# A four-mixer diffusion trunk on one core: a second buffer for the blocks that RWKV inverts, and its small weights packed into 512 columns

## The chip, the core and the metric

The kernel runs on one core of a Trainium2 chip. The metric is the device time of one execution in microseconds (us); lower is better. The engines of the core work side by side, each through its own queue in order: TensorE (PE, with its weight loads as PEld), VectorE (DVE), ScalarE (ACT), GpSimd (POOL), and SyncE (SP), which here issues nearly all DMAs.

## The reference, cut to what matters

Two layers. Each normalizes 1280 tokens (256 of context, 1024 latents; 1024 wide), projects them, and gives the columns to four mixers: S5, RWKV-7, retention (Ret) and gated linear attention (GLA). Each mixer scans the tokens forward and backward, and their outputs go together through an output projection, then an MLP. The change touches RWKV alone:

```
g = jax.nn.sigmoid(glo) @ g_up                                     # rank 64
w_raw = -softplus(-(w0[d] + jnp.tanh(wlo) @ w_up[d])) - 0.5        # rank 32, one per direction d
a = jax.nn.sigmoid(a0[d] + alo @ a_up[d])                          # rank 32
s = s * w_t + (s @ a_t) * b_t + v_t * k_t                          # 4 heads of 64, token by token
```

The kernel does the scan 64 tokens at a time (a chunk). Within a chunk the tokens depend on each other through a triangular matrix that has to be inverted; that is what "the inverse" means below.

## The kernel before, in words

**Stages.** Per layer: a first norm, the input projection together with S5, then the *head stage* (RWKV, Ret, GLA, and three parts of the modulation weights, `ada`), then output projection, second norm and MLP. In the profiled execution the head stage lies at about 461 to 1050 us in the first layer and 2500 to 3055 us in the second. All that the change does lies there.

**RWKV** works on 128 tokens of one direction, a *unit*; two units, one of each direction, make a *pair*, and there are ten pairs a layer (numbered 0 to 9 here). A pair passes through three steps:

- `unit1` (L361): loads the tokens' columns (`rw_zin`), multiplies the 128 rows `lo` with the small weights `rw_up` (L387 to 394; the result goes through ScalarE's tanh into `rw_l1` and `rw_ta`), and ends with the scores, `rw_TE` and `rw_TO`. `gate` (L481) is part of it for some units.
- `inv` (L506): stores the 32x32 diagonal blocks of the scores to DRAM (`rw_S`, L514: two stores from TE, two from TO), loads them back as `rw_B`, each block on four partitions (L518), and solves them in 31 steps on POOL, two instructions each (L527 `rw_tmp`, L528 `rw_Yv`). The result goes out in four stores (L531, `rw_S2`, which the profile writes `rw_S<-rw_Yv`) and comes back in four loads (L534) as `rw_DT`. I call these five kinds of DMA *score stores*, *B load*, *result stores* and *DT loads*.
- `unit2` and `chain` (L538, L582): the products with DT on TensorE, the state pass, the output.

`rw_B` has one buffer: the B load of pair n+1 waits for the last solving step of pair n. `rw_Yv`, `rw_S` and `rw_S2` have two buffers, DT, TE and TO three.

**Order.** `run` (L636) starts a pair every 6 rounds and its second part 12 rounds later, so `unit2` of pair n stands among the work of `unit1` of pair n+2. `merged` (L1996) mixes RWKV, Ret then GLA, and `ada`, each by its share of an estimate of TensorE's time (class `Pe`, L148), which counts a product half when its contraction has at most 64 rows. The tile framework then sets the order of each engine's queue by a model of its own. Both are done when the kernel is built; on the chip every queue runs in that fixed order.

Of the kernel before, what the change touches and what calls it, by code (L numbers as in the profile page):

```python
# [26 lines left out]
def _consts():  # L27
# [44 lines left out]
    dt = (i[None, :] - i[:, None]).astype(f)            # t - s  # L72
# [9 lines left out]
    ang = np.stack([(tt // 64).astype(f)[:, None] * inv, (tt % 64).astype(f)[:, None] * inv], 1)   # [SEQ, 2, 16]  # L82
# [14 lines left out]
# per-layer small parameters, one column block each (layout only)  # L97
# [3 lines left out]
def _cols(a):  # L101
    """[n*128] -> [128, n]"""
    a = np.asarray(a)
    return np.ascontiguousarray(a.reshape(-1, 128).T)
# [19 lines left out]
def lay_s5(inp, i):  # L124
    """[128, 4*512+64]: B (re; im), B (im; re), C (re; im), C (im; re) by state, and d on the diagonal of its group"""
# [11 lines left out]
def lay_rwup(inp, i):  # L137
    wu = np.asarray(inp["rw_w_up"][i])
    au = np.asarray(inp["rw_a_up"][i])
    gu = np.asarray(inp["rw_g_up"][i])  # L140
    z = np.zeros((128, 1280), np.float32)
    z[0:32, 0:512] = wu.transpose(1, 0, 2).reshape(32, 512)
    z[32:64, 512:1024] = au.transpose(1, 0, 2).reshape(32, 512)
    z[64:128, 1024:1280] = gu
    return z


class Pe:  # L148
    """the tensor engine, with an estimate of the time of what it was given (ns)"""
# [18 lines left out]
class K:  # L168
# [29 lines left out]
    def psum(self, **rings):  # L198
        """the banks of PSUM, shared out among kinds of users; b: the others"""
# [16 lines left out]
# ---------------------------------------------------------------- RWKV-7  # L216
def rw_mix(k, j, z, zm, mu, omu):
    """zm = z + mu*(shifted - z) for the 128 columns of tile j; z, zm [128, T]"""
# [42 lines left out]
RW_ROWS = 13            # rows of the spilled columns: v chunks swapped 2, kk 2, r 2, k 2, lo 1, v 2, v reversed by chunk 2  # L261


def rw_store(k, st, sm, omu, zrw, j, zt):
    """token shift of the 128 columns of tile j (zt [128, T]) and what the scans take from them, to DRAM;
    a generator: the parts that need the tensor engine come after the first step"""
# [45 lines left out]
class Rwkv:  # L312
    """zrw: DRAM [128, RW_ROWS, T] as rw_store leaves it; out(p, ps) takes the transposed output of 128 tokens"""

    R, LAT, NP = 6, 12, 3         # rounds between pairs, to their second part, pairs at a time
# [8 lines left out]
    def setup(self):  # L324
# [12 lines left out]
        # states and buffers with fixed zeros  # L337
# [15 lines left out]
        # by chunk: the first direction's output; what the normalized output is multiplied by, and what is added then  # L353
# [7 lines left out]
    def unit1(self, p, d, pr):  # L361
        """elementwise preparation, transposes, scores of 128 tokens in one direction"""
# [17 lines left out]
        def rev(ap):        # [.., 128] reversed in time for the backward direction  # L380
            return ap[..., ::-1] if d else ap

        def v4(ap):         # [128, 2, 128] -> [128, 2, c, 64]
            return ap.rearrange("p a (c t) -> p a c t", c=2)

        l1, ta = t("l1", [128, 2, 128]), t("ta", [128, 2, 128])
        for o, b, x in ((l1, self.w0h, 0), (ta, self.a0h, 512)):  # L387
            pw = k.ps("u1")
            for ti in range(2):
                cs = slice(x + d * 256 + ti * 128, x + d * 256 + ti * 128 + 128)  # L390
                PE.matmul(pw[:, ti * 128:ti * 128 + 128], self.wup[:, cs], lo, start=True, stop=True)
# [3 lines left out]
        # V (scan order, chunks swapped), token-major, into its place beside the chunk updates  # L395
# [11 lines left out]
        ec = self.ec[u["n"] % 2]        # decay from a chunk's start to before and, one column later, after a token  # L407
# [3 lines left out]
        # ar: (r~ 0 | a~ 0 | a~ 1 | r~ 1); a~ in scan order, r~ in natural order within its chunk  # L411
# [1643 lines left out]
```

## Time and profile before

| | us |
|---|---|
| median of 3 runs | 3920.55 (3920.0 to 3921.86) |
| span of the profiled execution | 3930.7 |
| head stage, first layer (461 to 1050) | about 589 |
| head stage, second layer (2500 to 3055) | about 555 |
| PE busy in the span | 3589.8 (91%) |
| POOL busy in the span | 1353.2 (34%) |

The profiled execution is known by its span, from the first to the last instruction; it is 10 us longer than the median, so a difference worked out on it is taken off the median. A busy share over the whole span hides that the stages differ: outside the head stage PE is nearly always busy, inside it is not. In the rows below, `psu` are the PSUM tiles of RWKV's products, `psb` those of most others. A wait in square brackets is the idle time of the engine just before the instruction, and what ended it.

### The profile page before, as it was taken

The numbers are of one execution on the slowest core, as the hardware profiler recorded it, in microseconds if no ns is written. First come the engines' busy times: TensorE is split into PE (matmuls) and PEld (weight loads), VectorE is DVE, ScalarE is ACT, GpSimd is POOL, SyncE is SP. The second block draws the span as 40 slices with busy tenths as digits, with TensorE's granted clock in tenths as the row PEclk, the third lists the DMA queues.
The fourth block names the chain that finished last, engine by engine and source line by source line (L and its number), as shares of the span: only waits on it lengthen the run. The fifth ranks groups of instructions, "written<-read, shape, count | busy, mean of one in ns | idle before, by whom it ended". The sixth has DMA issues, their size and how long they took to land.

```text
span 3930.7 us, 61448 instructions
## 1 busy us (share of the span) xinstructions
PE 3589.8 (91%) x23136; PEld 2973.0 (76%) x23136; DVE 2222.0 (57%) x4654; ACT 1475.3 (38%) x2980; POOL 1353.2 (34%) x2690
## 2 busy tenths in 40 slices
PE   6999888888799999999998999788888799999997
PEld 2998766577687888888886987667677678888885
DVE  5875456667555444444448875555667464444445
ACT  4266345755433111111214365346655332111222
POOL 1541256567431111111111451266676321111112
PEclk8999988787799999999999999898778899999998
DMA  5434575532521111111103434663423411111111
GB/s 184 149 111 145 163 210 141 168 92 61 163 89 33 33 44 33 43 33 44 33 27 120 146 115 144 180 177 112 111 73 96 141 54 49 49 43 43 49 53 43
DMA packets 369241, 372.84 MB, mean 95 GB/s; under 512 B 97360, under 2 KB 313104, under 8 KB 368688
## 3 DMA queue, kind: packets, MB, share of 16 engines
q1 hardware_dynamic: 333600, 343.08, 28.8%
q10 hardware_dynamic: 35344, 25.83, 2.1%
q8 instruction: 183, 3.00, 0.3%
q14 instruction: 114, 0.93, 0.1%
HBM read 285.18 MB, written 83.63 MB: 94 GB/s over the span
## 4 chain that ended last, share of the span: by engine, by line
PE 64%; POOL 9%; DMA 9%; DVE 8%; ACT 5%; issue 3%; SPq 1%; ACTq 0%; DVEq 0%; POOLq 0%
PE psb L161 56%; PE psu L161 5%; POOL rw_Yv L528 3%; POOL rw_tmp L527 3%; DMA rw_B<-rw_S 2%; DMA rw_S<-rw_Yv 1%; PE pss L161 1%; PE psfi L161 1%; DMA ada_w<-in_ada_w_dram 1%; DVE s_W L1158 1%; PE psch L161 1%; DVE n_h L1579 1%; DMA gl_v<-z_gvg 1%; DVE w_lo L1478 1%; DVE zm L223 1%
## 5 line engine op out<-in xcount | busy, mean ns | idle before, releaser
L161 PE MATMUL psb<-hh,w_hi 128*128 128x512 f32 (+1 forms) x1784 | 664.6, 374 | 12.9 <-ACT hh L1951 4.5
L161 PE MATMUL psb<-hl,w_hi 128*128 128x512 f32 (+1 forms) x1784 | 662.5, 372 | 6.5 <-DVE hl L1581 6.5
L161 PE MATMUL psb<-hh,w_lo 128*128 128x512 f32 (+1 forms) x1784 | 659.5, 371 | 0.0
L161 PE MATMUL psb<-mh,w_hi 128*128 128x512 f32 (+1 forms) x1600 | 601.2, 377 | 20.1 <-ACT w_hi L1475 15.3
L161 PE MATMUL psb<-mh,w_lo 128*128 128x512 f32 (+1 forms) x1600 | 598.3, 375 | 6.6 <-DVE w_lo L1478 6.6
L161 PE MATMUL psb<-ml,w_hi 128*128 128x512 f32 (+1 forms) x1600 | 600.5, 375 | 0.0
L1932 DVE SCALAR_TENSOR_TENSOR x<-psb,mod,x 128x512 f32<-128x512 f32 (+1 forms) x640 | 436.9, 694 | 273.8 <-PE psb L161 273.0
L1478 POOL TENSOR_TENSOR w_lo<-w_raw,w_hi 128x1024 fp32r<-128x1024 f32 x84 | 215.0, 2560 | 765.2 <-ACT w_hi L1475 574.8
L1950 DVE TENSOR_TENSOR hr<-hr 128x512 f32<-128x512 f32 x160 | 150.5, 941 | 513.6 <-ACT hr L1949 513.5
L1949 ACT ACTIVATE hr<-psb 128x512 f32<-128x512 f32 x160 | 88.7, 555 | 862.7 <-PE psb L161 861.8
L161 PEld LDWEIGHTS psb<-hh,w_hi 128*128 128x128 f32 x1784 | 338.6, 190 | 77.7 <-issue 6.0
L161 PEld LDWEIGHTS psb<-hl,w_hi 128*128 128x128 f32 x1784 | 338.0, 190 | 72.7 <-DVE hl L1581 11.0
L161 PEld LDWEIGHTS psb<-hh,w_lo 128*128 128x128 f32 x1784 | 337.5, 189 | 61.2 <-issue 1.4
L1952 POOL TENSOR_TENSOR hl<-hr,hh 128x512 fp32r<-128x512 f32 (+1 forms) x80 | 95.3, 1191 | 795.0 <-ACT hh L1951 502.9
L161 PEld LDWEIGHTS psb<-mh,w_hi 128*128 128x128 f32 x1600 | 303.7, 190 | 81.1 <-ACT w_hi L1475 17.4
L161 PEld LDWEIGHTS psb<-mh,w_lo 128*128 128x128 f32 x1600 | 303.3, 190 | 67.9 <-DVE w_lo L1478 8.2
L161 PEld LDWEIGHTS psb<-ml,w_hi 128*128 128x128 f32 x1600 | 303.4, 190 | 60.3 <-issue 2.9
L1475 ACT CAST w_hi<-w_raw 128x1024 fp32r<-128x1024 f32 (+1 forms) x208 | 212.8, 1042 | 317.8 <-PE psb L161 268.5
L527 POOL TENSOR_TENSOR rw_tmp<-rw_Yv,rw_B 128x60 f32<-128x60 f32 (+24 forms) x620 | 206.1, 332 | 198.6 <-DMA rw_B<-rw_S 100.0
L161 PE MATMUL psb<-w_hi,hh 128*128 128x256 f32 (+1 forms) x928 | 266.0, 290 | 4.8 <-ACT w_hi L1475 4.7
L161 PE MATMUL psb<-w_lo,hh 128*128 128x256 f32 (+1 forms) x928 | 266.9, 288 | 0.6 <-DVE w_lo L1478 0.6
L161 PE MATMUL psb<-w_hi,hl 128*128 128x256 f32 (+1 forms) x928 | 266.2, 288 | 0.0
(469 smaller groups left out, 6710.2 us busy)
## 6 DMA issues: line engine op xcount, KB each, us to landing
w_raw<-in_mlp_w_dram SPq DMA_DIRECT2D x128, 512.0 KB, 3.6
ada_w<-in_ada_w_dram SPq DMA_DIRECT2D x96, 512.0 KB, 4.4
w_raw<-in_w_in_dram SPq DMA_DIRECT2D x40, 512.0 KB, 5.6
w_raw<-in_w_out_dram SPq DMA_DIRECT2D x32, 512.0 KB, 5.2
rw_zin<-z_rw SPq DMA_DIRECT2D x20, 576.0 KB, 5.9
rw_B<-rw_S SPq DMA_DIRECT2D x20, 512.0 KB
z_rw<-zm SPq DMA_DIRECT2D x14, 640.0 KB, 3.1
x<-in_xT_dram SPq DMA_DIRECT2D x4, 2048.0 KB
```

Of the source, the lines that this page charges most:

```text
L161: return self.t.matmul(out, lhsT, rhs, **kw)
L223: nc.vector.scalar_tensor_tensor(dst[p0:p1], src[p0:p1], mu[p0:p1, j:j + 1], dst[p0:p1], op0=OP.mult, op1=OP.add)
L527: eng.tensor_tensor(o, bc(Yv[:, 0:m, s:s + 1], [128, m, n]), bc(B[:, s:s + 1, s + 1:32], [128, m, n]), op=OP.mult)
L528: eng.tensor_tensor(Yv[:, 0:m, s + 1:32], Yv[:, 0:m, s + 1:32], o, op=OP.add)
L1158: T_ = lambda o, a, b, op: V.tensor_tensor(o, a, b, op=op)
L1475: nc.scalar.copy(hi[:, :n], raw[:, :n])
L1478: e.tensor_tensor(lo[:, :n], raw[:, :n], hi[:, :n].bitcast(F32), op=OP.subtract)
L1579: nc.vector.scalar_tensor_tensor(h, x[:, kt], g[:, kt, cond:cond + 1], r[:, :n], op0=OP.mult, op1=OP.mult)
L1932: V.scalar_tensor_tensor(self.x[b][:, dt_], ps[:, :n], mod[:, 40 + dt_, cnd:cnd + 1], self.x[b][:, dt_], op0=OP.mult, op1=OP.add)
L1949: A.activation(r[:, :n], ps[:, :n], AF.Relu)
L1950: V.tensor_tensor(r[:, :n], r[:, :n], r[:, :n], op=OP.mult)
L1952: (G if j else V).tensor_tensor(hl[:, j, :n], r[:, :n], hh[:, j, :n].bitcast(F32), op=OP.subtract)
```

## The change

Beside comments, docstrings and blank lines that go, the diff is this:

```diff
 def lay_rwup(inp, i):
-    z = np.zeros((128, 1280), np.float32)
-    z[0:32, 0:512] = wu.transpose(1, 0, 2).reshape(32, 512)
-    z[32:64, 512:1024] = au.transpose(1, 0, 2).reshape(32, 512)
-    z[64:128, 1024:1280] = gu
+    z = np.zeros((128, 512), np.float32)
+    z[0:32] = wu.transpose(1, 0, 2).reshape(32, 512)
+    z[32:64] = au.transpose(1, 0, 2).reshape(32, 512)
+    z[64:128, 0:256] = gu
...
     def unit1(self, p, d, pr):
-        for o, b, x in ((l1, self.w0h, 0), (ta, self.a0h, 512)):
-            pw = k.ps("u1")
-            for ti in range(2):
-                cs = slice(x + d * 256 + ti * 128, x + d * 256 + ti * 128 + 128)
-                PE.matmul(pw[:, ti * 128:ti * 128 + 128], self.wup[:, cs], lo, start=True, stop=True)
+        pws = [k.ps("u1"), k.ps("u1")]
+        for ti in range(2):
+            for x, pw in enumerate(pws):
+                cs, s = slice(d * 256 + ti * 128, d * 256 + ti * 128 + 128), slice(32 * x, 32 * x + 32)
+                PE.matmul(pw[:, ti * 128:ti * 128 + 128], self.wup[s, cs], lo[s], start=True, stop=True)
+        for o, b, pw in ((l1, self.w0h, pws[0]), (ta, self.a0h, pws[1])):
             for ti in range(2):
                 c = d * 2 + ti
                 A.activation(rev(o[:, ti]), pw[:, ti * 128:ti * 128 + 128], AF.Tanh, ...
...
     def gate(self, p, zin):
-        PE.matmul(pg[:, 0:256], lo, self.wup[:, 1024:1280], start=True, stop=True)
+        PE.matmul(pg[:, 0:256], lo[64:128], self.wup[64:128, 0:256], start=True, stop=True)
...
     def inv(self, pr):
-        B = w.tile([128, 32, 32], F32, name="rw_B", bufs=1)
+        B = w.tile([128, 32, 32], F32, name="rw_B", bufs=2)
-        tmp = w.tile([128, 256], F32, name="rw_tmp", bufs=1)
+        tmp = w.tile([128, 76], F32, name="rw_tmp", bufs=1)
```

Per partition `rw_B` takes 4096 bytes more, `rw_up` 3072 and `rw_tmp` 720 less. The products with the small weights have 32 rows of contraction in place of 128 (64 in `gate`), so `Pe` counts them half. Line numbers behind L387 grow by one. The order of the queues changes inside the two head stages; three places follow.

SP's queue, first layer, the score stores (`rw_S<-rw_TE`, `rw_TO`) and the B load of pair 4 and the result stores (`rw_S2<-rw_Yv`) of pair 3. Before:

```order
L514 DMA rw_S_7417<-rw_TE_7234 32x8x32 x2
L514 DMA rw_S_7417<-rw_TO_7235 32x8x32 x2
L754 DMA gl_g_8680<-z_gvg0_398 128x256
L917 DMA z_gk0_396<-gl_c_7539 128x257
L917 DMA z_gk0_396<-gl_c_7540 128x257
L899 DMA gl_L_7639<-z_ga0_397 16x256
L917 DMA z_gk0_396<-gl_c_7600 128x257
L917 DMA z_gk0_396<-gl_c_7601 128x257
L899 DMA gl_L_7688<-z_ga0_397 16x256
L518 DMA rw_B_7422<-rw_S_7417 128x1x1024
L531 DMA rw_S2_6840<-rw_Yv_6775 256x1x32 x4
```

The same place in the change:

```order
L515 DMA rw_S_7353<-rw_TE_7161 32x8x32 x2
L515 DMA rw_S_7353<-rw_TO_7162 32x8x32 x2
L519 DMA rw_B_7358<-rw_S_7353 128x1x1024
L607 DMA rw_dY_4776<-rw_Y_7434 128x256
L374 DMA rw_zin_8470<-z_rw0_393 128x9x128
L532 DMA rw_S2_6764<-rw_Yv_6699 256x1x32 x4
```

The B load moved up to its score stores, and other DMAs now stand between it and the result stores of the pair before.

SP's queue, first layer, score stores and B load of pair 8, result stores and DT loads (`rw_DT`) of pair 7. Before:

```order
L514 DMA rw_S_10906<-rw_TE_10648 32x8x32 x2
L514 DMA rw_S_10906<-rw_TO_10649 32x8x32 x2
L518 DMA rw_B_10911<-rw_S_10906 128x1x1024
L531 DMA rw_S2_10188<-rw_Yv_10123 256x1x32 x4
L754 DMA gl_g_10231<-z_gvg0_398 128x256
L799 DMA gl_L_10233<-z_gq0_395 128x128
L534 DMA rw_DT1_4764<-rw_S2_10188 32x8x32 x4
```

The same place in the change:

```order
L532 DMA rw_S2_9918<-rw_Yv_9853 256x1x32 x2
L615 DMA rw_YQ_11098<-rw_dY_4776 128x768
L535 DMA rw_DT1_4764<-rw_S2_9918 32x8x32 x4
L524 DMA rw_Yv_11471<-in_consts_dram 128x256
L755 DMA gl_g_9615<-z_gvg0_398 128x256
L800 DMA gl_L_9617<-z_gq0_395 128x128
L755 DMA gl_c_10028<-z_gk0_396 128x385
L515 DMA rw_S_10632<-rw_TE_10371 32x8x32 x2
L515 DMA rw_S_10632<-rw_TO_10372 32x8x32 x2
L519 DMA rw_B_10637<-rw_S_10632 128x1x1024
```

The score stores and the B load moved behind the result stores and the DT loads of the pair before.

POOL's queue, first layer, the end of the solving steps of pair 7 and the first of pair 8 (`128x31`). Before:

```order
L527 TENSOR_TENSOR rw_tmp_10124<-rw_Yv_10123,rw_B_10121 128x8
L528 TENSOR_TENSOR rw_Yv_10123<-rw_Yv_10123,rw_tmp_10124 128x8
L725 TENSOR_TENSOR gl_nth_9905<-gl_nth_9905,gl_lng_7524 128x256
L527 TENSOR_TENSOR rw_tmp_10914<-rw_Yv_10913,rw_B_10911 128x31
L528 TENSOR_TENSOR rw_Yv_10913<-rw_Yv_10913,rw_tmp_10914 128x31
L808 TENSOR_TENSOR gl_L_10233<-gl_c_10224 128x64
```

In the change, the last of 18 instructions that stand there:

```order
L812 TENSOR_TENSOR gl_L_9617<-gl_c_9608 128x2x32
L809 TENSOR_TENSOR gl_L_9617<-gl_c_9608 128x4x16
L810 TENSOR_TENSOR gl_L_9617<-gl_c_9608 128x4x16
L811 TENSOR_TENSOR gl_L_9617<-gl_c_9608 128x4x16
L812 TENSOR_TENSOR gl_L_9617<-gl_c_9608 128x4x16
L809 TENSOR_TENSOR gl_L_9617<-gl_c_9608 128x8x8
L810 TENSOR_TENSOR gl_L_9617<-gl_c_9608 128x8x8
L811 TENSOR_TENSOR gl_L_9617<-gl_c_9608 128x8x8
L812 TENSOR_TENSOR gl_L_9617<-gl_c_9608 128x8x8
L528 TENSOR_TENSOR rw_tmp_10640<-rw_Yv_10639,rw_B_10637 128x31
```

GLA's elementwise work of one chunk stood between the solving steps of pair 8 and now stands ahead of them.

## Rows read from the trace of the kernel before

**Rows 1.** The page's head, then the chain of waits by line, head stages of both layers

```profile
span 3930.7 us, 61448 instructions
...
by line: PE psu L161 14.6%; POOL rw_tmp L527 7.8%; POOL rw_Yv L528 7.5%; PE psb L161 6.5%; issue 6.1%; DMA rw_B<-rw_S 4.6%; PE psfi L161 4.1%; DMA rw_S<-rw_Yv 4.1%; DMA ada_w<-in_ada_w_dram 3.4%; PE psch L161 2.4%; DMA z_mix<-rw_mix 2.0%; P
...
by line: PE psu L161 16.2%; POOL rw_Yv L528 10.7%; DMA rw_B<-rw_S 10.0%; POOL rw_tmp L527 9.9%; issue 5.9%; PE psb L161 5.3%; DMA rw_S<-rw_Yv 3.6%; DMA rw_DT<-rw_S 2.5%; PE psfi L161 2.5%; PE psch L161 2.2%; DMA gl_v<-z_gvg 2.2%; SPq L531 2
```

**Rows 2.** POOL around the end of inverse 0, in time: start, length, engine, line

```profile
560.67 0.47 POOL L528 TENSOR_TENSOR rw_Yv<-rw_Yv,rw_tmp 128x8 f32<-128x8 f32 x1
...
569.46 0.24 POOL L527 TENSOR_TENSOR rw_tmp<-rw_Yv,rw_B 128x31 f32<-128x31 f32 x1 [5.11 <-DMA rw_B<-rw_S]
```

**Rows 3.** Windows of POOL over gaps between inverses: length, busy (instructions); three sets

```profile
701.94:714.41 12.47, 0.17 (x4) 0.50 0.35 95
...
2637.39:2651.87 14.48, 8.30 (x18) 0.93 0.47 106
...
sum 81.06, POOL 19.07; mean POOL 2.72
...
847.56:864.24 16.68, 4.87 (x17) 0.69 0.35 89
...
sum 47.71, POOL 6.32; mean POOL 1.58
...
sum 68.56, POOL 2.21; mean POOL 0.32
```

**Rows 4.** SP's queue in time: score stores of pairs 1 and 4, B load of 1

```profile
529.51 0.95 SPq L514 DMA_DIRECT2D rw_S<-rw_TO  x2
...
560.62 0.55 SPq L518 DMA_DIRECT2D rw_B<-rw_S  x1
...
683.80 0.89 SPq L514 DMA_DIRECT2D rw_S<-rw_TO  x2
```

**Rows 5.** SP's queue in time: pair 7 after inverse 6; stores after inverse 7

```profile
847.59 2.52 SPq L531 DMA_DIRECT2D rw_S<-rw_Yv  x4
850.15 0.60 SPq L514 DMA_DIRECT2D rw_S<-rw_TO  x1
...
852.70 2.58 SPq L534 DMA_DIRECT2D rw_DT<-rw_S  x4
...
856.29 0.56 SPq L518 DMA_DIRECT2D rw_B<-rw_S  x1
...
900.81 2.81 SPq L531 DMA_DIRECT2D rw_S<-rw_Yv  x4
...
909.83 1.80 SPq L534 DMA_DIRECT2D rw_DT<-rw_S  x4
```

**Rows 6.** Windows by stage: length, PE, PEld, DVE, ACT, POOL busy, granted clock

```profile
510.00:710.00 200.00, 163.22 (x1159) 126.49 (x1159) 117.08 (x313) 103.93 (x270) 131.11 (x342) 0.86 0.54 156
710.00:1010.00 300.00, 264.47 (x3258) 219.47 (x3257) 212.06 (x573) 179.61 (x488) 209.05 (x607) 0.78 0.38 106
2550.00:2750.00 200.00, 173.12 (x1174) 132.65 (x1173) 112.86 (x303) 101.46 (x266) 128.88 (x354) 0.87 0.51 147
2750.00:3030.00 280.00, 233.42 (x2945) 204.78 (x2945) 192.74 (x508) 162.55 (x447) 191.28 (x546) 0.76 0.31 82
```

**Rows 7.** PE in time: small weights (128 rows), then Ret (64 rows), then `ada`

```profile
532.35 0.71 PE L161 MATMUL psu<-rw_zin,rw_up 128*128 128x128 f32 x4
532.99 0.72 PE L161 MATMUL psb<-rt_qt,rt_kt 64*128 64x128 f32 x8
533.64 1.03 PE L161 MATMUL psfi<-ada_w,condsl 128*2 128x512 f32 x4
```

**Rows 8.** The chain of waits in time, start of the head stages

```profile
461.24 3.79 DMA rw_up<-in_rwup_dram
...
2503.19 6.86 DMA rw_zin<-z_rw
```

## The prediction

> **What bounds the kernel now.** I read the page first, then the chain of waits cut to the two head stages, because the diff touches nothing outside them. The page says how long the profiled execution is: 3930.7 us [rows 1]. That is 10 us above the median of 3920.55; every sum below is a difference on the profiled execution and is taken off the median. In the head stages the chain passes through TensorE's RWKV products, the solving steps on POOL (15% and 21% of the stage, two lines each), and a DMA, `rw_B<-rw_S`, with 4.6% and 10.0% [rows 1]. These shares are of windows of 592 and 570 us, so the B load has 27 and 57 us of the chain. This is the most the chain could lose by it, if nothing else were late next.
>
> Then POOL in time. Inverse 0 ends at 561.14 (560.67 + 0.47), inverse 1 starts at 569.46, and its wait is for the B load [rows 2]. SP issued that load at 560.62, although the last score stores of pair 1 were issued at 529.51 [rows 4]: with one buffer it had to wait for the last solving step. So each pair has a gap on POOL in which a 9 us load runs and little else. The 18 gaps between the inverses of both layers come to 197 us (81.06 + 47.71 + 68.56), in which POOL works 28 (19.07 + 6.32 + 2.21) [rows 3]. That idle time, 170 us over both layers, is what is at stake.
>
> Third, the windows by stage: PE is busy 834 of 980 us (163.22 + 264.47 + 173.12 + 233.42) [rows 6]. So PE leaves 146 us; a gain of 170 can't be had, one of 30 to 70 can.
>
> **The change part by part: the second buffer.** It lets the B load start when its own score stores have landed. Whether it does depends on where SP's fixed queue has it, so I sort the 18 gaps by the order of the change and by when the scores come in the trace.
>
> (a) *Seven gaps (before pairs 1, 2, 4 of the first layer, 1, 2, 3, 6 of the second): the load stands ahead of the earlier pair's result stores, and the scores are early.* Pair 1's last score stores leave 31 us before the inverse ahead of it ends [rows 2, 4]; the latest of the seven are pair 4's, 18 us ahead (683.80 against 701.94 [rows 3, 4]). From the last score store to the first solving step pair 7 needs 14.1 us (850.15 of [rows 5] to 864.24 of [rows 3]). So the data are there and the gap closes. Idle now: 81.06 - 19.07 = 62 us [rows 3]. Left: half a microsecond each, and some 5 us before pair 2, half of whose scores now stand behind `unit2` of pair 0 on PE. Gain 62 - 3 - 5 = 54 us. The 19 us of other POOL work in these gaps is still to be done.
>
> (b) *Four gaps (before pairs 5 and 7; 4 and 7): the load stands early, but the scores are late.* Pair 7's last score store leaves at 850.15 [rows 5], the inverse ahead ends at 847.56 [rows 3]; in the other three it leaves at most 12 us ahead. Here the 14 us of stores, load and waits pass whatever the buffer; the idle 47.71 - 6.32 = 41 us [rows 3] stays, moved earlier with the rest. Gain 0, at most 41.
>
> (c) *Seven gaps (before pairs 3, 6, 8, 9; 5, 8, 9): the score stores now stand behind the earlier pair's result stores, four of them behind its DT loads too.* This is the part that speaks against the change. Before, one gap has just this order: pair 7 after inverse 6 (it counts in set (b) by its new place). There the result stores go out at 847.59, the last score store at 850.15, the DT loads at 852.70, the B load at 856.29 [rows 5], and the gap is 16.68 us where the others of set (c) have 68.56 / 7 = 9.8 [rows 3]. For the three that have one pair of score stores ahead of the DT loads I take 16.7; for the four that have both behind them I add those loads and the stores, 2.6 + 1.7, and get 21. Sum 3 x 16.7 + 4 x 21 = 134 us. The order of POOL moves 84 other instructions out of the inverses into these gaps (7, 0, 18, 18; 7, 16, 18); at 0.38 us (8.30 + 4.87 us for 18 + 17 [rows 3]) that is 32 us of work that no longer lengthens an inverse. So idle 134 - 32 = 102 against 68.56 - 2.21 = 66 now: a loss of 36 us. The ends: a loss of nothing if a gap stays at 9.8, of 60 if the result stores take as long to land as after inverse 7 (909.83 - 903.62 = 6.2 us, against 852.70 - 850.11 = 2.6 [rows 5]), since 7 x 3.6 = 25 come on top.
>
> (d) *The results come back sooner.* After inverse 7 the B load was sent just ahead of the result stores, and the DT loads could go 6.2 us after the last of these; after inverse 6, with no B load ahead, after 2.6 [rows 5]. Now no B load is sent at that moment, so `unit2` gets its DT some 3.6 us sooner. It counts where `unit2`, and `unit1` behind it, is what the next inverse waits for: the four gaps of (b) and the two ends of stage, 6 x 3.6 = 22 us. I take 10, since PE has other work queued there; ends 0 and 22.
>
> **The small weights.** Their load is 0.26 MB in place of 0.66. On the chain of the first layer it has 3.79 us [rows 8]; at the same rate 2.3 go. In the second it lies ahead of the chain's 6.86 us load of `rw_zin` [rows 8], and up to as much goes. I take 3 in all. No row shows a product of 32 rows with 128 columns. Four products of 128 rows start 0.64 us before the next group, 160 ns each; the eight 64-row products behind them, two halves of the array by turns, take 0.65, 81 ns each, the change of shape at both ends included [rows 7]. With the 64-row price four take 0.32 less a group; 40 groups give 13 us of PE time. The other end is no gain, or a loss of the same size if two 32-row products don't overlap. Most of it lies where PE has a wait behind it anyway; I take 2.
>
> At this point the Trainium skill speaks against the edit: "TensorEngine Tiling (Array Packing)", Key Properties, says that changing the tiling mode drains the engine, and each of these groups now changes it twice. Here the rows disagree as to size: the 64-row group pays both changes within its 81 ns each. By the rule alone, with a drain of one group's 0.3 us, the 40 groups would lose 12 us of PE time in place of gaining 13.
>
> `gate`'s product keeps its 256 columns and runs alone: nothing. The smaller `rw_tmp` costs nothing; the largest step needs 76 columns. That `Pe` counts less makes RWKV stand a little earlier among Ret, GLA and `ada`; the work is the same.
>
> **The sum.** -54 + 0 + 36 - 10 - 3 - 2 = -33. 3920.55 - 33 = 3888 us.
>
> **The rivals.**
>
> *All gaps close (faster).* If the scores in set (c) are ready only when the queue takes them, their place costs nothing, and the pieces I call late are just PE's own pace: (c) is 0, and (d) counts in full: -54 + 0 - 22 - 3 - 2 = -81, which is over half of PE's 146 idle us; with 20 given back to PE's queue -61, 3860 us. For it: the queue is made with a model in which stores stand when their data come. Against it: before, in every gap of (c) the stores left ahead of the result stores.
>
> *SP's queue becomes the bound (slower).* The result stores of an inverse and the score stores of the next pair are now one chain on SP, and the loads of `rw_zin` for the pair after stand behind them. Price: the late gaps at their far end (-54 + 60), nothing from (d), and the gain of (a) halved since the next pair's scores start later: -27 + 60 = +33, less 5 for the weights: 3948 us. It decides from the point at which the seven gaps average over 24 us: (134 + 33) / 7. For it: SP waits in order, and all other loads with it. Against it: the one gap of this order measured 16.68.
>
> *PE is the bound (no change).* PE is busy 88% of 710 to 1010 [rows 6] and works in order. If its queue there is what is slow, the gains of the second halves are waits that move from POOL to PE, and only pairs 1 and 2 of each layer give something, about as much as (c) takes: 3917 us.
>
> *The change doesn't do what it says*: excluded for the buffer, since in 11 of 18 gaps the load has moved ahead of the result stores.
>
> **How the numbers follow.** Forecast 0.52 (3888, by itself 3868 to 3906), all gaps close 0.18, SP's queue 0.17, PE 0.13. The range goes to the first rival's 3860 and some 10 below, and towards the slower one's until a tenth is left out: 3850 to 3930. Within 0.2% (8 us) counts as no change, which is about what a measurement can tell here. Faster: 0.52 + 0.18 and a little of PE's case, 0.72; same 0.12; slower 0.16.
>
> **What would show it.** Right: the POOL windows of the seven gaps of (a) drop to about 1 us, those of (c) grow to 17 to 21 and hold the other POOL work, and no B load is left on the chain in (a); the wait from the result stores to the DT loads drops to under 3 us; a group of four small products takes about 0.35 us. Wrong: gaps in (c) under 10 (first rival) or above 24 (second), or the gaps of (a) closed and the stage as long as before, with PE's waits for `rw_DT` grown (third).

## The result, and the profile after

The change made the kernel slower: 3975.76 us, median of four runs (3963.14 to 3982.85), against 3921.2 for the kernel before, ratio 1.0135, 95% interval 1.0112 to 1.0159. Forecast were 3888 us and a range up to 3930.

The profiled execution of the changed kernel is 50.4 us longer than that of before:

```profile
span 3981.1 us, 61419 instructions
```

First, windows by stage as in [rows 6], but each span is cut where the load of `rw_up` (start of a head stage) and the first load of the output projection's weights (its end) are issued. The columns are length, busy time of PE, PEld, DVE, ACT and POOL with their instructions, granted TensorE clock, DMA share, GB/s. Before:

```profile
461.20:1051.60 590.40, 491.34 (x4978) 392.56 (x4978) 387.43 (x1035) 320.80 (x863) 371.25 (x1005) 0.81 0.49 142
2499.90:3062.50 562.60, 455.14 (x4430) 372.47 (x4430) 359.71 (x943) 297.23 (x803) 346.94 (x952) 0.81 0.45 126
0.00:461.20 461.20, 413.18 (x2634) 351.01 (x2634) 290.44 (x755) 216.24 (x355) 133.45 (x264) 0.96 0.44 140
1051.60:2499.90 1448.30, 1400.04 (x7606) 1197.51 (x7606) 777.40 (x1429) 434.58 (x684) 314.46 (x372) 0.98 0.23 71
3062.50:3930.70 868.20, 830.12 (x3488) 659.46 (x3488) 407.03 (x494) 206.47 (x275) 187.08 (x101) 0.97 0.18 58
```

and the changed kernel:

```profile
467.00:1094.50 627.50, 518.85 (x4978) 408.37 (x4978) 388.20 (x1034) 318.19 (x859) 364.76 (x1004) 0.77 0.47 131
2534.60:3116.30 581.70, 471.57 (x4430) 381.12 (x4430) 356.86 (x943) 298.39 (x803) 332.30 (x952) 0.75 0.43 121
0.00:467.00 467.00, 415.40 (x2634) 352.98 (x2634) 287.51 (x755) 216.13 (x355) 132.96 (x264) 0.96 0.43 139
1094.50:2534.60 1440.10, 1392.84 (x7606) 1192.67 (x7606) 780.18 (x1430) 435.48 (x686) 314.10 (x372) 0.98 0.23 72
3116.30:3981.00 864.70, 825.28 (x3488) 660.69 (x3488) 407.11 (x494) 206.47 (x275) 186.88 (x101) 0.98 0.18 58
```

The head stages grow by 37.1 and 19.1 us; the rest is +5.8 ahead of them (nothing there is touched, and in five of the other traces the first head stage starts 3.3 to 4.6 us late too) and -8.2 and -3.5 behind them. Look at PE's busy time, the second column. TensorE issues as many instructions as before, 4978 and 4430, yet is busy 27.5 and 16.4 us longer. So 44 of the stages' 56 us is an equal number of instructions that take longer, and the clock says how: 0.81 and 0.81 became 0.77 and 0.75. The clock has two levels, 1.2 and 2.4 GHz, so the mean gives the time at the lower one: 2 x 0.19 x 590.4 = 224 us before, 2 x 0.23 x 627.5 = 289 now; in the second layer 214 and 291. Counted over the traces' records, PE was busy at the lower level for 174 and 166 us before and for 229 and 214 now; half of that growth is 52 us, which covers the 44. PE's idle time grew by 9.6 and 2.7 only.

Second, the gaps between inverses on POOL, which answer to [rows 3], in the sets (a), (b), (c) of the prediction (the last line is the twenty inverses themselves):

```profile
sum 6.20, POOL 0.69; mean POOL 0.10
...
sum 20.93, POOL 5.16; mean POOL 1.29
...
sum 183.68, POOL 26.16; mean POOL 3.74
...
sum 795.15, POOL 596.11; mean POOL 29.81
```

(a) went from 81.06 us to 6.20, as forecast; (b) from 47.71 to 20.93, better; (c) from 68.56 to 183.68, 26.2 each where 19 were forecast. The sum of all three is 210.81 us, where it was 197 before: the gaps moved and grew. This is how such a place looks in SP's queue, to be read beside [rows 5]: the last score store of pair 6 and its B load leave behind the result stores (L532) and DT loads (L535) of pair 5 (one line of each is shown):

```profile
801.21 0.57 SPq L532 DMA_DIRECT2D rw_S<-rw_Yv  x1
...
803.60 1.27 SPq L535 DMA_DIRECT2D rw_DT<-rw_S  x1
...
807.85 0.43 SPq L515 DMA_DIRECT2D rw_S<-rw_TO  x1
...
810.54 0.56 SPq L519 DMA_DIRECT2D rw_B<-rw_S  x1
```

Third, PE's groups in the head stages; behind the bar stand busy time, mean ns of one record (a float32 product leaves two) and the idle time just before. Before, first layer, then second:

```profile
L161 PE MATMUL psu<-rw_R,rw_DT 128*128 128x128 f32 x320 | 55.5, 334 | 24.6 <-DMA rw_DT<-rw_S 22.7 <-DVE rw_R L558 1.9
L161 PE MATMUL psfi<-ada_w,condsl 128*2 128x512 f32 x192 | 49.9, 663 | 8.7 <-DMA ada_w<-in_ada_w_dram 8.6
...
L161 PE MATMUL psu<-rw_R,rw_DT 128*128 128x128 f32 x320 | 62.0, 360 | 31.2 <-DMA rw_DT<-rw_S 31.1
L161 PE MATMUL psb<-gl_v,gl_kt 128*32 128x64 f32 x144 | 6.1, 245 | 3.2 <-DMA gl_v<-z_gvg 2.2 <-ACT gl_mix L1713 0.9
```

The changed kernel:

```profile
L161 PE MATMUL psfi<-ada_w,condsl 128*2 128x512 f32 x192 | 58.8, 685 | 33.9 <-DMA ada_w<-in_ada_w_dram 33.8
L161 PE MATMUL psu<-rw_R,rw_DT 128*128 128x128 f32 x320 | 56.4, 333 | 6.1 <-DMA rw_DT<-rw_S 5.9 <-DVE rw_R L559 0.3
...
L161 PE MATMUL psu<-rw_R,rw_DT 128*128 128x128 f32 x320 | 55.9, 334 | 6.7 <-DMA rw_DT<-rw_S 6.3 <-DVE rw_R L559 0.3
L161 PE MATMUL psb<-gl_v,gl_kt 128*32 128x64 f32 x144 | 6.8, 272 | 20.2 <-DMA gl_v<-z_gvg 12.5 <-ACT gl_mix L1714 6.1 <-ACT gl_kt L764 1.5
```

The gaps that the second buffer was to close are closed, and PE's wait for the DMA of DT fell by 16.8 and 24.8 us, 42 in all. That the buffer did it can be seen in the second layer only: the kernel with the packing and one buffer, below, has this wait at 6.1 and 35.0 us, where it is 5.9 and 6.3 here and was 22.7 and 31.1 before. The wait for `ada`'s weights rose by 25.2 in the first layer and the idle time ahead of GLA's products `gl_v,gl_kt` by 17.0 in the second: PE's queue is in a fixed order, and it stood still at another place. (The chain of waits of this trace breaks off at 3116.87 us, so it can't be set beside [rows 1].)

### The profile page after: what moved, and what is told of

It is laid out like the page before. It is cut to its first block, busy times and chain, and to the rows that moved or that the text cites. A ratio compares the mean times of both kernels' runs of the same rounds, so it can differ in the third digit from the quotient of the medians.

```text
span 3981.1 us, 61419 instructions
## 1 busy us (share of the span) xinstructions
PE 3623.9 (91%) x23136; PEld 2995.8 (75%) x23136; DVE 2219.9 (56%) x4654; ACT 1474.7 (37%) x2978; POOL 1331.0 (33%) x2690
## 5 line engine op out<-in xcount | busy, mean ns | idle before, releaser
L1950 ACT ACTIVATE hr<-psb 128x512 f32<-128x512 f32 x160 | 88.5, 554 | 858.5 <-PE psb L161 857.6
L528 POOL TENSOR_TENSOR rw_tmp<-rw_Yv,rw_B 128x60 f32<-128x60 f32 (+24 forms) x620 | 195.1, 315 | 166.5 <-DMA rw_B<-rw_S 41.5
```

Of the source, the lines that this page charges most:

```text
L528: eng.tensor_tensor(o, bc(Yv[:, 0:m, s:s + 1], [128, m, n]), bc(B[:, s:s + 1, s + 1:32], [128, m, n]), op=OP.mult)
L1950: A.activation(r[:, :n], ps[:, :n], AF.Relu)
```

## The experiments

All were timed against the kernel before on the same chip; its medians there were 3921 to 3928 us. "Clock" is the range of the mean granted clock over the timed runs, "stages" the lengths of the two head stages in the profiled one.

| kernel | us | ratio (95%) | clock | stages |
|---|---|---|---|---|
| changed | 3975.76 | 1.0135 (1.0112, 1.0159) | 0.912 to 0.916 | 627.5, 581.7 |
| packing, one buffer | 3988.04 | 1.0155 (1.0135, 1.0174) | 0.910 to 0.914 | 646.4, 577.1 |
| changed, old cost | 3972.46 | 1.0114 (1.0096, 1.0132) | 0.915 to 0.916 | 638.2, 567.2 |
| results on ACT's queue | 3993.43 | 1.0170 (1.0153, 1.0187) | 0.911 to 0.914 | 635.2, 577.7 |
| results on POOL's queue | 3973.66 | 1.0111 (1.0086, 1.0136) | 0.912 to 0.919 | 625.3, 576.2 |
| before, light cost | 3948.46 | 1.0069 (1.0053, 1.0084) | 0.925 to 0.927 | 613.8, 565.1 |
| before, 32 rows | 3992.37 | 1.0184 (1.0162, 1.0207) | 0.910 to 0.917 | 611.9, 598.7 |
| program order, 128 rows | 4207.58 | 1.0738 (1.0714, 1.0762) | 0.898 to 0.902 | 714.3, 665.6 |
| program order, 32 rows | 4219.10 | 1.0757 (1.0736, 1.0777) | 0.888 to 0.892 | 720.4, 675.9 |

**Which half of the change.** Theories: SP's queue (1), the order that lighter costs bring (2), the 32-row products (3), waits that move from the gaps into the inverses (4). The packing alone, with `rw_B` at `bufs=1` and `rw_tmp` at 256 columns:

> The change without its second buffer (rw_B with one buffer, rw_tmp with 256 columns as before): the packed weights, the 32-row products and the lighter counting of their cost alone. Theory 1 (the harm is SP's in-order queue, where score stores and B loads now stand behind the earlier pair's result stores): with one buffer the B load waits for the last solving step again, the eighteen gaps between inverses sum to about 190 to 215 us and the time is 3915 to 3935 us. Theory 2 (the harm is the order that the lighter costs give, which leaves the last GLA chunks behind the last unit2 at the end of the first layer): the first out-projection is late by 20 us as in the changed kernel, 3940 to 3960. Theory 3 (the 32-row products themselves are slow): 3950 to 3980, with these products at over 160 ns each.

It is as slow as the whole change: the packing alone is enough for the harm, 64 us by the medians. The changed kernel's median is 12 us lower, but the intervals overlap, so that the second buffer gives anything back is not shown. Then the old cost:

```diff
                 PE.matmul(pw[:, ti * 128:ti * 128 + 128], self.wup[s, cs], lo[s], start=True, stop=True)
+                PE.cost += 4 * 128 / 2.4 * 0.5
...
         PE.matmul(pg[:, 0:256], lo[64:128], self.wup[64:128, 0:256], start=True, stop=True)
+        PE.cost += 4 * 256 / 2.4 * 0.5
```

> The changed kernel, but the products with the packed weights and gate's product are counted at their old cost in the merge of RWKV with Ret, GLA and ada, so that it goes nearly as before the change. Theory 1 (SP's queue): 3965 to 3985, late gaps still 24 to 28 us each. Theory 2 (the lighter costs shift the order): 3915 to 3940, the end of the first layer's stage back by about 20 us. Theory 3: as the changed kernel, 3976.

No difference from the changed kernel that the intervals show. (The scheduler's own model still sees other products, so before's order doesn't come back.) Its second stage is worth a look:

```profile
2542.20:3109.40 567.20, 457.85 (x4430) 369.27 (x4430) 356.48 (x943) 299.44 (x805) 338.85 (x952) 0.80 0.45 124
```

With 32-row products the clock there is 0.80 and PE is busy 458 us, where before had 0.81 and 455. Its first stage has 0.74. So the order has a part in what 32-row products cost.

**SP's queue.** The result stores and DT loads go to ScalarE's queue, or the result stores alone to POOL's:

```diff
-            nc.sync.dma_start(S2[:, :, :, j].rearrange("x b i t -> (x b) i t"), Yv[32 * j:32 * j + 32])
+            nc.gpsimd.dma_start(S2[:, :, :, j].rearrange("x b i t -> (x b) i t"), Yv[32 * j:32 * j + 32])
```

> The changed kernel with the result stores and the DT loads issued by ScalarE on its own queue, so that no score store and no B load stands behind them on SP. Theory 1 (SP's queue): the seven late gaps fall from 26 us on average to under 12, some 100 us of gaps go, of which a third to a half reaches the end: 3900 to 3945. Theory 2 (order): gaps fall but the stages end no sooner, 3960 to 3985. Theory 4 (the end of an inverse is set by PE and by POOL's own waits, so that what a gap loses the inverse before or after it gains): the sum of the inverses' own lengths grows by what the gaps lose, 3950 to 3985.

> The changed kernel with the result stores alone issued by POOL, the engine that makes the results; DT loads, score stores and B loads stay on SP, where the B loads then stand early for all pairs. Theory 1 (SP's queue): late gaps under 12 us, 3890 to 3940 us. Theory 2 (order): 3950 to 3985. Theory 4 (waits move into the inverses): 3950 to 3985, the sum of the inverses' lengths above the changed kernel's 795 us by what the gaps lose.

Theory 1 falls: neither is faster. The windows of the second, first over its 18 gaps, then over its 20 inverses:

```profile
sum 122.27, POOL 57.19; mean POOL 3.18
...
sum 878.31, POOL 631.56; mean POOL 31.58
```

The gaps of all sets lost 88.5 us (210.81 in the changed kernel), the inverses grew by 83.2 (795.15 there), as theory 4 has it. Of the 83.2, POOL's own work is 35.5 (631.56 for 596.11) and waiting 47.7. POOL takes its queue in order too, and what it no longer waits for in the gaps it waits for inside the inverses, in part at instructions of other mixers. One of its groups in that kernel between 569.22 and 862.86, idle time behind the bar:

```profile
L1018 POOL TENSOR_TENSOR rt_vd<-rt_v,rt_GV 128x256 f32<-128x256 f32 x4 | 2.5, 614 | 19.9 <-DMA rt_v<-z_ret 19.9
```

This wait was not new: over the first head stage the group waits 33.0 us here, 27.0 in the changed kernel. The late gaps of (c) were not what set the time.

**Order against rows.** The kernel before with the lighter cost only, and the kernel before with only the 32 rows (64 in `gate`) that are not zero, cost restored:

```diff
+                PE.cost -= 4 * 128 / 2.4 * 0.5
```

```diff
-                PE.matmul(pw[:, ti * 128:ti * 128 + 128], self.wup[:, cs], lo, start=True, stop=True)
+                q = slice(0, 32) if x == 0 else slice(32, 64)
+                PE.matmul(pw[:, ti * 128:ti * 128 + 128], self.wup[q, cs], lo[q], start=True, stop=True)
```

> The kernel before, with nothing changed but the estimate: the products with the small weights and gate's product are counted half, as after the change. All 128-row products, the one buffer and the wide weights stay; only the order of the queues moves. Seen so far in all four kernels with packed weights: the head stages have as many TensorE instructions as before (4978 and 4430), but TensorE is busy for 20 to 47 us longer in the first, and its granted clock there is 0.74 to 0.77 where it was 0.81. Theory order (a queue order without the gaps and cover of before's lengthens the stage, and the clock follows): 3945 to 3990, clock in the first head stage under 0.78. Theory rows (products on 32 rows lower the granted clock, whatever the order): 3910 to 3935, clock 0.80 to 0.82.

> The kernel before with its wide weights, one buffer and its loop order, but the products with the small weights take only the 32 rows that are not zero (gate's 64), and are counted at their old cost. The queues still move, since the scheduler's model sees other products. Theory rows: the granted clock in the first head stage is 0.74 to 0.77, 3955 to 3990. Theory order: undecided by itself, as its order is neither before's nor the change's: 3915 to 3990.

The first, by windows of its two stages:

```profile
462.10:1075.90 613.80, 490.13 (x4978) 393.12 (x4978) 386.59 (x1034) 315.31 (x859) 369.94 (x1004) 0.80 0.48 135
2518.00:3083.10 565.10, 450.05 (x4430) 370.52 (x4430) 354.68 (x943) 299.98 (x805) 337.84 (x952) 0.80 0.46 126
```

TensorE's busy time is that of before (490 for 491, 450 for 455) and so is the clock; the stage is 23 us longer by idle time. So order alone costs: the time is what the theory of order gave, the clock what the theory of rows gave. The 32-row kernel, with wide weights and one buffer:

```profile
460.40:1072.40 612.00, 503.70 (x4978) 394.78 (x4978) 389.29 (x1035) 318.61 (x861) 357.39 (x1005) 0.79 0.48 137
2516.40:3115.10 598.70, 472.23 (x4430) 378.36 (x4430) 357.73 (x943) 299.72 (x805) 336.08 (x952) 0.77 0.43 119
```

Its clock is lower, though in the first stage less than the 0.74 to 0.77 that was expected, and of the 58 us by which its stages are longer PE's busy time is 29; the rest is idle time, and its order differs too. To take the order out, the kernel before and this one were built with the queues in the order of the program (`schedule_with_timeline_sim=False`); then every queue of the two is the same, and 178 products differ (four in each of 40 units, and 18 of `gate`; the expectation counts 176 groups):

> The kernel before with its queues in the order in which the program is written, not in the order of the scheduler's model. A base line for the next kernel: 3950 to 4150.

> The products on 32 rows (64 in gate) of the kernel two places ahead, with the queues in the order of the program: every queue has exactly the order of the base line, and only the 176 groups of products with the small weights differ. Theory rows: slower than the base line by 25 to 70 us, granted clock in the head stages lower by 0.03 to 0.07, TensorE busier by 15 to 40 us. Theory order: within 8 us of the base line and the same clock, or faster by up to 13 us.

Windows of the head stages with 128 rows:

```profile
496.30:1210.60 714.30, 515.69 (x4978) 392.29 (x4978) 377.37 (x1031) 321.67 (x861) 357.99 (x1002) 0.77 0.42 117
2685.20:3350.80 665.60, 478.60 (x4430) 377.41 (x4430) 346.54 (x940) 306.76 (x809) 336.30 (x950) 0.75 0.38 106
```

and with 32 rows:

```profile
494.80:1215.20 720.40, 541.65 (x4978) 402.75 (x4978) 377.14 (x1031) 321.99 (x861) 355.64 (x1002) 0.73 0.42 116
2690.50:3366.40 675.90, 498.57 (x4430) 386.00 (x4430) 346.95 (x939) 307.79 (x809) 338.96 (x949) 0.72 0.38 105
```

In the same order the clock falls from 0.77 and 0.75 to 0.73 and 0.72, and PE is busy 26 and 20 us longer. The four timed clocks of the two don't overlap. The times do (4204.72 to 4222.38, 4215.49 to 4224.44): this order leaves PE 199 and 187 us idle, and of 46 us more busy time 11 to 15 reach the end, less than the 25 expected. The kernel before leaves it 99 and 107.

As the order is the same, the records of the two traces can be laid side by side (ten of the second layer stand swapped). The small products, `gate` and the two records behind each group take 5.8 and 4.2 us more in the two layers; all other records 20.2 and 15.7. Those of the others that ran at the same level in both traces differ by 1.3 and 0.0 us. So 36 of the 46 us fall on products that nobody touched, and among them on those that ran at another level of the clock.

Where the clock parts can be seen at the first group of a stage. PE in time, then 5 us windows (columns as above), 128 rows:

```profile
506.78 2.07 PE L161 MATMUL psu<-rw_zin,rw_up 128*128 128x128 f32 x8 [8.64 <-DMA ada_w<-in_ada_w_dram]
...
505.00:510.00 5.00, 3.22 (x12) 2.16 (x14) 1.18 (x3) 1.74 (x6) 1.38 (x3) 0.50 1.09 341
510.00:515.00 5.00, 4.44 (x24) 2.09 (x20) 4.06 (x11) 4.83 (x15) 1.40 (x6) 0.83 0.69 226
515.00:520.00 5.00, 3.68 (x21) 2.27 (x20) 4.67 (x10) 3.86 (x12) 4.30 (x8) 1.00 0.16 54
```

and 32 rows:

```profile
505.91 1.23 PE L161 MATMUL psu<-rw_zin,rw_up 32*128 32x128 f32 x8 [9.05 <-DMA ada_w<-in_ada_w_dram]
...
505.00:510.00 5.00, 3.38 (x14) 1.32 (x14) 2.02 (x5) 2.52 (x8) 0.55 (x2) 0.50 1.04 325
510.00:515.00 5.00, 4.29 (x18) 1.69 (x17) 3.18 (x9) 4.08 (x13) 1.61 (x7) 0.50 0.48 147
515.00:520.00 5.00, 5.00 (x19) 3.98 (x18) 3.29 (x8) 2.26 (x7) 1.59 (x3) 0.50 0.08 23
520.00:525.00 5.00, 5.00 (x12) 1.32 (x10) 2.77 (x10) 2.36 (x6) 3.37 (x5) 0.50 0.53 149
525.00:530.00 5.00, 4.48 (x32) 3.21 (x31) 3.15 (x11) 1.20 (x4) 1.41 (x3) 0.79 0.60 187
```

Both begin at the lower level after an idle stretch. Behind the 128-row group the clock is up again in the window from 510; behind the 32-row group, which is itself 0.84 us shorter, the windows from 510, 515 and 520 are at 1.2 GHz with PE about as busy or busier, and it rises 15 us later. This is one place; the stages' means above are over all of them.

**How many rows.** In program order again: the four products of a unit on 32 rows and `gate` on 128; and the four on 64 rows, half of them zero weights.

> The base line in program order, with the four products per unit on 32 rows alone; gate's product keeps its 128 rows. Every queue in the base line's order. If these products lower the clock, it is as with both changed: mean clock 0.887 to 0.893 over the run, 4214 to 4224 us. If gate's 64 rows do: as the base line, 0.900 and 4208.

> The base line in program order, with the four products per unit on 64 rows, 32 of them zero weights; gate's product keeps its 128 rows. If what counts is how many rows of the array work: between the two, 0.893 to 0.898 and 4210 to 4217 us. If it is that two row groups of 32 work side by side or that the mode changes: as the base line.

The clocks were 0.889 to 0.894 and 0.891 to 0.895, against 0.898 to 0.902 and 0.888 to 0.892 above; 4217.3 and 4222.11 us (ratios 1.0733 and 1.0749, intervals of 0.005) don't tell any of the four apart. So the four products on 32 rows make most of the drop, without `gate`. With 64 rows it is about as large: the two stages of the profiles have 0.75 and 0.74, with 32 rows 0.75 and 0.71, and the timed clocks overlap, so a step between is not shown. That two groups of 32 rows work side by side is not needed for it, since the 64-row products don't. Whether the number of rows counts or the change of shape stays open: products on 64 rows among products on 128 change the shape as well.

**The second buffer without the packing.** It fits if two other tiles give up a buffer:

```diff
-        cs = t("cs", [128, 2, 128])
-        bk = t("bk", [128, 2, 4, 64])
+        cs = t("cs", [128, 2, 128], 1)
+        bk = t("bk", [128, 2, 4, 64], 1)
```

In the second kernel `ar` takes the place of `bk`; in three more Ret's and GLA's share in the first layer's merge is 95 or 90 for 75, or RWKV's 170 for 165.

> The second buffer without the packing: the kernel before with its wide weights and 128-row products, rw_B with two buffers and rw_tmp with 76 columns; the room comes from rw_bk and rw_cs, which get one buffer in place of two. Theory clock and order (the harm is the lower granted clock that the 32-row products leave, and the order that their lighter cost brings; the buffer by itself helps a little): granted clock in the head stages 0.80 or above, TensorE busy 485 to 500 and 445 to 460 us in them, 3895 to 3935 us, depending on where the scheduler puts GLA's last chunks. Theory buffer (the second buffer itself costs, by score stores behind result stores): 3945 to 3985 at a clock of 0.80 or above.

> As the kernel ahead of it, but the room comes from rw_ar and rw_cs: the same work in another order of the queues. Theory clock and order: clock as there, 3895 to 3940 us; what it differs from the kernel ahead of it by is the worth of order alone, up to 25 us. Theory buffer: 3945 to 3985.

> Second buffer, 128-row products, the small buffers as in the kernel with rw_bk and rw_cs single; in the first layer the share of Ret and GLA in the merge is 95 in place of 75, so that GLA's last chunks are not left behind RWKV's last unit2. Theory clock and order: the first head stage loses its tail (590 to 600 us in place of 613), clock 0.92 or above: 3895 to 3930 us. Where order is only luck: 3920 to 3975.

> As the kernel ahead of it, with RWKV's share in the first layer 170 in place of 165 and Ret and GLA at 75: a small change, and a queue in which the last RWKV products alternate with GLA's. Theory clock and order: 3895 to 3935 us. Where order is only luck: 3920 to 3975.

> Second buffer and 128-row products, rw_bk and rw_cs single, share 90 of Ret and GLA in the first layer, where 95 gave 3929. Theory clock and order: 3895 to 3930 us, clock 0.925 or above. Where order is only luck: 3920 to 3980.

| 128 rows, two buffers | us | ratio (95%) | clock | stages |
|---|---|---|---|---|
| `bk`, `cs` single | 3940.96 | 1.0033 (1.0020, 1.0045) | 0.921 to 0.930 | 612.7, 548.8 |
| `ar`, `cs` single | 3981.42 | 1.0134 (1.0104, 1.0164) | 0.921 to 0.926 | 595.1, 614.1 |
| `bk`, `cs`; share 95 | 3928.91 | 1.0006 (0.9991, 1.0022) | 0.927 to 0.933 | 598.1, 553.6 |
| `bk`, `cs`; RWKV 170 | 3961.34 | 1.0079 (1.0051, 1.0106) | 0.922 to 0.924 | 609.4, 579.4 |
| `bk`, `cs`; share 90 | 3950.89 | 1.0060 (1.0041, 1.0078) | 0.922 to 0.928 | 619.7, 569.0 |

Nearly the same work in five orders spreads over 52 us. None is faster than before, and four are slower by their intervals. Only the share of 95 came out as theory clock and order has it, and there luck's range holds it too; the time of `ar`, `cs` lies in the range of theory buffer. So what the second buffer is worth by itself is not shown: the orders differ, and the two tiles that gave up a buffer may cost something as well. The idea that the tail of GLA decides was not borne out: shares 95 and 90 differ by 22 us in the first stage.

All five keep a mean clock above 0.920, where no kernel with 32-row products and nothing added, six of them in orders of their own, came over 0.919. PE's busy time in the two stages together is 919 to 972 us with 128 rows (before, light cost, these five) and 976 to 1002 in the six with 32. In single stages order alone does as much, here the first of share 90 and the second of `ar`, `cs`:

```profile
465.10:1084.90 619.80, 513.89 (x4978) 407.20 (x4978) 390.15 (x1035) 317.61 (x861) 362.92 (x1005) 0.79 0.49 136
...
2499.50:3113.60 614.10, 474.95 (x4430) 385.67 (x4430) 359.46 (x943) 305.76 (x809) 343.41 (x953) 0.76 0.43 116
```

They have the clock at 0.79 and 0.76 and PE 23 and 20 us busier than before without any 32-row product. The second has the most idle time of PE of all these stages, 139 us, but the first has only 106, so idle time by itself doesn't explain it.

**Giving the clock something back.** Added products of 128 rows that nothing reads, four a unit: behind each 32-row product in program order; behind each pair of them; and in the changed kernel behind each group of four.

```diff
+        for ti in range(2):
+            for pw in pws:
+                PE.t.matmul(pw[:, 256 + ti * 128:384 + ti * 128], vs[:, ti], k.ident, start=True, stop=True)
```

> The kernel with 32-row products in program order, and behind each of these products an added one of 128 rows and 128 columns into a part of the same PSUM tile that nothing reads (160 in all, some 26 us of TensorE work by the 0.64 us that four such took). Theory clock: the time at the lower clock in the two head stages falls from 406 and 406 us to under 385 each and the mean clock rises from 0.889 to 0.895 or more, so the added work costs less than it takes: 4205 to 4225 us. Rival (the rows do not matter for the clock): clock 0.889, 4225 to 4245.

> The changed kernel, and behind each group of four 32-row products four added ones of 128 rows and 128 columns that nothing reads. More TensorE work by some 26 us, nothing taken away. Theory clock: the time at the lower clock in the head stages falls from 304 and 307 us to about 250 to 280, mean clock from 0.912 to 0.917 to 0.925, and the kernel is not slower than the changed one, 3935 to 3975 us. Rival (order or the buffer, not the clock): 3980 to 4005 at 0.912.

> As the kernel in program order with an added product behind each 32-row product, but the added ones stand behind each pair of 32-row products, so that rows change half as often. There the two groups of products together took 67 us more of TensorE in the first layer, 0.84 us for each added product. If the changes between 32 and 128 rows are what that cost: 30 to 40 us more in place of 67, the clock rises to 0.893 or more, 4215 to 4232 us. If the added work itself is: 60 us or more, 4240 to 4250.

The last first. The changed kernel with 160 products added took 3978.3 us (ratio 1.0127, 1.0102 to 1.0152), not told apart from the time without them, at a clock of 0.924 to 0.930, which none of the packed kernels had reached. Its stages:

```profile
461.20:1056.40 595.20, 507.16 (x5138) 402.24 (x5138) 386.66 (x1034) 320.24 (x861) 360.93 (x1004) 0.85 0.47 132
2511.30:3107.10 595.80, 482.88 (x4590) 392.44 (x4590) 353.39 (x943) 299.30 (x803) 342.49 (x952) 0.80 0.44 118
```

In the first stage PE does 160 records more and is busy 11.7 us less, and the stage is 32 us shorter; in the second the clock returns too (0.80 for 0.75), but the stage is 14 us longer. Why the time doesn't fall is in the rows of the added products, first layer, then second:

```profile
L394 PE MATMUL psu<-c_ident,rw_zin 128*128 128x128 f32 x160 | 34.1, 348 | 0.0
...
L394 PE MATMUL psu<-c_ident,rw_zin 128*128 128x128 f32 x160 | 36.4, 361 | 0.0
```

They take 70 us, not the 26 expected: a float32 product leaves two records, and the four records that took 0.64 us in [rows 7] are two products. Without them PE would be busy for 920 us in the stages (507.16 + 482.88 - 70.5), less than before's 946. The clock gives back about what the added work takes.

In program order the test failed: 4244.1 us at 0.890 to 0.899 and 4234.37 at 0.892 to 0.895, above 4219.10 and 0.888 to 0.892 without additions. The second lies between the two ranges that were expected for it. Rows of the first layer say why, product by product:

```profile
L393 PE MATMUL psu<-c_ident,rw_zin 128*128 128x128 f32 x160 | 52.8, 426 | 0.0
L161 PE MATMUL psu<-rw_zin,rw_up 32*128 32x128 f32 x160 | 51.7, 417 | 10.6 <-DMA rw_zin<-z_rw 7.7 <-ACT rw_ta L397 1.4 <-ACT rw_R L480 1.4
```

and pair by pair:

```profile
L161 PE MATMUL psu<-rw_zin,rw_up 32*128 32x128 f32 x160 | 40.3, 389 | 10.5 <-DMA ada_w<-in_ada_w_dram 8.2 <-ACT rw_VT L404 2.2
L395 PE MATMUL psu<-c_ident,rw_zin 128*128 128x128 f32 x160 | 39.9, 391 | 0.0
```

With 160 changes between 32 and 128 rows the two groups take 104.5 us, with 80 changes 80.2: 0.30 us a change. These changes and the added products themselves, 40 to 55 us in a layer, are more than the clock gave.

## Why the prediction was wrong

- *"I take 2"* for the small weights, ends +13 and -13, is the step that failed. It priced these products by their own time alone and put what they do to all other products at nothing. The runs showed that behind 32-row products TensorE's clock is lower and the others take longer: 44 us more of PE's busy time in the head stages of the changed kernel, more than three times the worse end. That 32-row products lower the clock is shown at a fixed order, where 36 of 46 us more fell on products that nobody touched; how the 44 us divide between them and the new order, which alone moved single stages by 20 and 23 us, is not settled.
- The priced part was small. [rows 7] was misread: its four and eight records are two and four products, so by that reading a unit would have saved 0.64 us and 40 units 26, not 13. At the fixed order the small products took 53.5 us for 62.1 over both layers; in the changed kernel 60.3 for 60.2. The first group's 1.23 us for 2.07, both at the lower clock, is not typical.
- The Trainium skill ("TensorEngine Tiling (Array Packing)", Key Properties) says that a change of the tiling mode drains TensorE; the prediction put this at 12 us, 0.3 for each of 40 groups. The trace agrees that a change costs something, 0.30 us each, and with two a group that makes 24 us. It is not most of the loss: at the fixed order the records next to the changes, the small products, `gate` and the two records behind each group, grew by 10 us of the 46.
- *"The work is the same"*, for the lighter cost: the lighter cost alone makes the kernel before 26 us slower, by idle time, at an unchanged clock.
- *"That idle time, 170 us over both layers, is what is at stake"*: (a) closed as said, and PE waits 42 us less for DT, though in the first layer the packing with one buffer does the same. But PE's idle time in the stages did not fall, and where the gaps closed almost all the inverses grew. A gap on POOL with a load in it was not on the path that sets the end; my third rival, PE's own queue, was nearer in mechanism than in time.
- (c) was mis-sized, 26.2 us a gap for 19, above the 24 at which I let SP's queue decide. The runs that took the stores off SP were no faster, so that rival falls, though its 3948 us was the nearest number; that was luck.
- (d) came true where it was looked at: at pair 5 the first DT load goes 1.8 us after the last result store (803.60 less 801.78), under the 3 forecast.
- The weights' load, 3 us: from its issue to the first inverse 51.8 and 48.8 us passed before, 53.8 and 45.9 now. Nothing to be seen in sum.

Left open: what in 32-row products lowers the clock, rows or change of shape; why `ada`'s loads come later; and whether any order with two buffers beats the kernel before, as the best tried is not told apart from it.

## What to carry to other kernels

A product with fewer rows isn't cheaper by its own row alone: read the granted clock of the stretch behind it, and the busy time of all the other products, which here grew by more than the edit could ever save. Before a gap on one engine is priced as gain, check that PE's idle time has the same gap; what moves into another wait is not won. Where a scheduler sets the order, run the change once in a fixed order: an edit of the cost alone moved this kernel by 26 us. And find out how many records of the profile one product leaves before pricing by them.

## What was not expected of the hardware

In the same order of the queues, four products a unit on 32 rows in place of 128 left TensorE at 1.2 GHz for longer: mean clock 0.73 for 0.77 in the first head stage. Added 128-row products, which took 70 us of TensorE themselves, brought it from 0.77 to 0.85 in the first stage of the changed kernel, and the time stayed the same. And changing between 32 and 128 rows took 0.28 to 0.30 us each time in the two layers of the runs in program order.
